# Strassen factors of a SwiGLU's w_down formed further ahead, and part of VectorE's work given to GpSimd

## The chip, the cores and the metric

The kernel runs on one core of a Trainium2 chip. The metric is the device time of one execution in microseconds: the median of three runs of the kernel before is 3245.2 us (3243.39 to 3246.24). TensorE (PE), VectorE (DVE), ScalarE (ACT) and GpSimd (POOL) each run their own list of instructions in a fixed order; SyncE (SP) and POOL issue the DMAs. An instruction that waits holds back everything behind it on its own engine.

## The reference

One layer of a decoder trunk on x of 2048 rows and 1024 columns, in float32, and a final norm:

```
h   = RMSNorm(x);  P = h @ W_in
A   = short gated convolution branch
B   = sparse attention: indexer scores I[t,s]; each query keeps the 256 best causal keys,
      softmax over them with a relative-position bias
m   = sigmoid(g_a) * y_a + sigmoid(g_b) * y_b
x   = x + m @ W_out
x   = x + (silu(h2 @ W_gate) * (h2 @ W_up)) @ W_down,   h2 = RMSNorm(x),  D_FF = 2816
out = RMSNorm_final(x)
```

The change concerns the last product, `@ W_down`, and the accumulation into x.

## The kernel before

The sequence is cut in two halves of 1024 rows. In order of time the program makes the projections and the indexer's scores for all rows, then for half 0 and after it for half 1: the attention, the branches and W_out, and the SwiGLU (MLP). The MLP of half 0 lies at about 1308 to 2029 us of the profiled run, that of half 1 at about 2535 to 3229 us.

Every float32 product is made of three matmuls on a high and a low part of each factor (`mm3`, L154). `split_w` (L128) makes the parts: ACT copies the high part (L129), and DVE or POOL subtracts it from the raw tile for the low part (L130).

The MLP takes the 22 tiles of 128 columns of D_FF in 11 pairs. `gate_up` (L932) computes one tile: 96 matmuls into PSUM tiles `gu`, a tanh on ACT (L945) and two operations on DVE (L946, L947) that leave the hidden tile `th`. The w_down product of a pair is a 2 by 2 block product, and for the first ten pairs it is made with seven products in place of eight (`PRODUCTS`, L975). Three of them (m3, m6, m5) are issued among the matmuls of the same pair's second gate_up, four (m2, m7, m4, m1) among those of the next pair's first one; `between` spreads them. Each product needs two factors: `hid`, a sum of two hidden tiles made by POOL (L964), and `wd`, a sum of two blocks of w_down made by DVE (L964), each then split in high and low (L129 on ACT, L130 on POOL for hid, on DVE for wd). The factors of one product are summed and split in one go, one product ahead. Each product has four PSUM tiles `dn` (four buffers), and DVE adds each of them to one or two blocks of the accumulator x2 (L1008). Since the products are shared out so, one block of x2 carries a combination of the others: `corner` (L1033) sets it up before the first pair and resolves it ahead of the last, by 12 operations on DVE each time (L1037). The last pair is made the ordinary way (L1064).

Half 0's MLP has a second task. The keys of the 128-row blocks 15 to 10, which half 1's attention needs, are selected by bisection as background work (priority lowered by `LOW`). Per block DVE prepares 16-bit keys (`descend_act`, L381 to L384), ACT runs 17 steps, each a sign count over the whole row (L358), then its sign (L367) and the next threshold (L369); DVE prepares the lower 16 bits (from L393 to L401), ACT runs 16 more steps, and DVE makes the threshold (L410 to L415) and the mask (`topk`, L425 to L448). Then the keys of the next block can follow. The first operations of half 1's attention (matmul L638, DVE L641) stand behind this on DVE.

The order on each engine is made by a scheduler from the order of emission and the priorities, so moving an emission moves instructions on several engines.

Of the kernel before, what the change touches and what calls it, by code (L numbers as in the profile page):

```python
# [25 lines left out]
P = 128  # L26
# [16 lines left out]
FB = 3  # L43
RAWB = (4, 4)
# [30 lines left out]
def trunk_kernel(tc, x, g_mix, w_in, b_gate, conv_w, w_a, w_b, w_out, rel_bias,  # L75
# [677 lines left out]
    for half in (0, 1):  # L753
# [206 lines left out]
        def combine(tag, bufs, eng, op, a, b=None):  # L960

            if b is not None:
                ab = ci.tile([P, CH], F32, name=tag, tag=tag, bufs=bufs)
                eng.tensor_tensor(ab, a, b, op=op)  # L964
                a = ab
            hi = ci.tile([P, CH], F32R, name=tag, tag=tag, bufs=bufs)
            lo = ci.tile([P, CH], F32R, name=tag, tag=tag, bufs=bufs)
            split_w(hi, lo, a, eng)
            return hi, lo
# [15 lines left out]
        def operands(name, A, B):  # L985

            def term(get, tag, bufs, eng, spec):
                if len(spec) == 1:
                    return combine(tag, bufs, eng, None, get(*spec[0]))
                return combine(tag, bufs, eng, spec[1], get(*spec[0]), get(*spec[2]))  # L990
            left, right = PRODUCTS[name][:2]
            return (term(lambda i, e: A[i, e], "hid", 8, nc.gpsimd, left),
                    term(lambda e, n: B[2 * e + n], "wd", 7, nc.vector, right))
# [39 lines left out]
        def corner(plus, minus):  # L1033

            for x0, x1 in zip(x2[0:4], x2[4:8]):
                for part, op in ((x1[:, 0:CH], plus), (x0[:, 0:CH], minus), (x0[:, CH:D], minus)):
                    nc.vector.tensor_tensor(x1[:, CH:D], x1[:, CH:D], part, op=op)  # L1037

        corner(ADD, SUB)
        held = None  # L1040
        for fpair in range(NF // 2):
# [4 lines left out]
            last = fpair == NF // 2 - 1  # L1046
            A, hid = {}, {}
            if held:
                begin(strassen(("m2", "m7", "m4", "m1"), *held), 16)
            if last:  # L1050
                gate_up(fpair, 0, lambda i, th: hid.update({(i, 0): combine("hid", 8, nc.gpsimd, None, th)}))
                drain()
                corner(SUB, ADD)
                B = down_rows(fpair)
                gate_up(fpair, 1, lambda i, th: hid.update({(i, 1): combine("hid", 8, nc.gpsimd, None, th)}))
                for n in range(2):
                    ns = slice(n * CH, (n + 1) * CH)
                    wd = [combine("wd", 7, nc.vector, None, B[2 * e + n]) for e in range(2)]
                    for tt in range(8):
# [5 lines left out]
                        if half == 1 and n == 1:  # L1065
                            finish(tt, x2[tt])
                break
# [6 lines left out]
            begin(strassen(("m3", "m6", "m5"), A, B), 12)  # L1074
# [44 lines left out]
```

## Time and profile before

| | |
|---|---|
| median of three runs | 3245.2 us |
| the profiled execution | 3246.63 us, its span 3244.9 us |
| PE busy | 3137.3 us, 97% of the span |
| DVE, ACT, POOL busy | 2154.5, 1947.2, 1023.0 us |
| mean granted clock of PE | 0.987 |

Busy shares are means over stages with different limits. In what follows a stage is read by its windows, by the waits of PE, and by the chain of ACT and DVE that the background search forms. A row of a timeline ends, where its engine stood idle, with the idle time and what ended it.

### The profile page before, as it was taken

To read this page: it belongs to the slowest core of one execution; us is meant where nothing else is said; L and a number is where in the kernel's file an instruction comes from. 1 tells how busy PE (TensorE), PEld (TensorE's weight loads), DVE (VectorE), ACT (ScalarE), POOL (GpSimd) and SP (SyncE) were. 2 spreads that over 40 slices of the span, in tenths; PEclk is the share of its full clock that TensorE was granted. 3 is DMA by queue.
4 is the path that set the end of the run, shared out by engine and by line. 5 is a ranking of instruction groups with operands and counts; after the bars stand their busy time and mean duration, and the time that the engine had idled before them with its cause. 6 is when DMAs were issued, how large, how long until landed. Compare 5 with 4: busy or idle time off the path is not lost. (4 is left out here: it accounts for less than half of the span.)

```text
span 3244.9 us, 42086 instructions
## 1 busy us (share of the span) xinstructions
PE 3137.3 (97%) x14483; PEld 2582.6 (80%) x14483; DVE 2154.5 (66%) x3762; ACT 1947.2 (60%) x3794; POOL 1023.0 (32%) x844
## 2 busy tenths in 40 slices
PE   8999999999999899899999999799999999999998
PEld 6788888888887678787878788587788788888886
DVE  6344356663527764878697987899863676667666
ACT  6479888779757785584848568677732322222222
POOL 5411122221114421344344433122221344344342
PEclk9999999999999999999999999899999999999999
DMA  7644333332334871322122225213372411111111
GB/s 226 178 136 127 94 95 97 96 99 90 104 112 108 221 256 46 92 68 87 51 84 70 89 63 140 71 53 79 102 248 65 143 65 53 46 59 46 46 46 52
DMA packets 338639, 324.82 MB, mean 100 GB/s; under 512 B 20340, under 2 KB 268360, under 8 KB 338040
## 3 DMA queue, kind: packets, MB, share of 16 engines
q1 hardware_dynamic: 301800, 293.64, 29.4%
q0 software_dynamic: 36624, 28.48, 4.3%
q8 instruction: 114, 1.87, 0.3%
q14 instruction: 101, 0.83, 0.1%
HBM read 248.09 MB, written 75.54 MB: 100 GB/s over the span
## 5 line engine op out<-in xcount | busy, mean ns | idle before, releaser
L1008 DVE SCALAR_TENSOR_TENSOR x<-dn,x 128x512 f32<-128x512 f32 x800 | 511.5, 683 | 201.4 <-PE dn L157 201.3
L358 ACT ACTIVATE dump<-key,nt 128x384 uint8<-128x384 int16 (+27 forms) x420 | 548.8, 1307 | 10.3
L155 PE MATMUL gu<-h2hi,wgu 128*128 128x512 f32 x1408 | 549.9, 391 | 0.1
L156 PE MATMUL gu<-h2lo,wgu 128*128 128x512 f32 x1408 | 549.2, 390 | 0.0
L157 PE MATMUL gu<-h2hi,wgu 128*128 128x512 f32 x1408 | 548.8, 390 | 0.0
L155 PE MATMUL mm<-hThi,whi 128*128 128x512 f32 (+2 forms) x1216 | 472.2, 389 | 1.2 <-ACT hThi L149 1.2
L157 PE MATMUL mm<-hThi,wlo 128*128 128x512 f32 (+2 forms) x1216 | 470.5, 388 | 0.8 <-POOL wlo L130 0.8
L156 PE MATMUL mm<-hTlo,whi 128*128 128x512 f32 (+2 forms) x1216 | 470.4, 387 | 0.0
L130 POOL TENSOR_TENSOR wlo<-raw,whi 128x512 fp32r<-128x512 f32 (+1 forms) x132 | 179.4, 1360 | 671.1 <-ACT whi L129 574.3
L266 DVE SCALAR_TENSOR_TENSOR acc<-r,iwT,acc 128x512 f32<-128x512 f32 (+2 forms) x266 | 196.2, 738 | 277.0 <-ACT r L261 275.7
L130 POOL TENSOR_TENSOR wgu<-raw,wgu 128x1024 fp32r<-128x1024 f32 x88 | 224.1, 2549 | 289.6 <-ACT wgu L129 280.9
L155 PEld LDWEIGHTS gu<-h2hi,wgu 128*128 128x128 f32 x1408 | 265.4, 188 | 56.1 <-DVE h2lo L150 0.7
L156 PEld LDWEIGHTS gu<-h2lo,wgu 128*128 128x128 f32 x1408 | 265.4, 189 | 55.1
L157 PEld LDWEIGHTS gu<-h2hi,wgu 128*128 128x128 f32 x1408 | 265.1, 188 | 55.3
L157 PEld LDWEIGHTS mm<-hThi,wlo 128*128 128x128 f32 (+1 forms) x1216 | 226.7, 187 | 50.6 <-POOL wlo L130 1.2
L155 PE MATMUL dn<-wd,hid 128*128 128x512 f32 x624 | 245.2, 393 | 17.8 <-ACT hid L129 10.3
L155 PEld LDWEIGHTS mm<-hThi,whi 128*128 128x128 f32 (+1 forms) x1216 | 226.8, 187 | 43.3 <-ACT hThi L149 1.4
L156 PEld LDWEIGHTS mm<-hTlo,whi 128*128 128x128 f32 (+1 forms) x1216 | 226.9, 187 | 42.6
L156 PE MATMUL dn<-wd,hid 128*128 128x512 f32 x624 | 244.5, 392 | 0.0
L157 PE MATMUL dn<-wd,hid 128*128 128x512 f32 x624 | 235.3, 392 | 1.1 <-POOL hid L130 1.0
L964 POOL TENSOR_TENSOR hid<-th 128x512 f32<-128x512 f32 x100 | 144.0, 1440 | 289.6 <-DVE th L947 282.9
L129 ACT ACTIVATE hid<-hid 128x512 fp32r<-128x512 f32 x100 | 62.8, 628 | 240.4 <-POOL hid L964 240.3
(210 smaller groups left out, 6315.0 us busy)
## 6 DMA issues: line engine op xcount, KB each, us to landing
raw<-in_w_in_dram SPq DMA_DIRECT2D x124, 256.0 KB
raw<-in_w_ffn_gate_dram SPq DMA_DIRECT2D x44, 512.0 KB
raw<-in_w_ffn_up_dram SPq DMA_DIRECT2D x44, 512.0 KB
rawd<-in_w_ffn_down_dram SPq DMA_DIRECT2D x44, 512.0 KB
S<-SD SPq DMA_DIRECT2D x80, 256.0 KB
GT<-f SPq DMA_DIRECT2D x64, 256.0 KB
ta<-GT SPq DMA_DIRECT2D x64, 256.0 KB
S<-SD SPq DMA_DIRECT2D x68, 192.0 KB
```

What stands on the lines that cost most here:

```text
L129: nc.scalar.activation(hi, raw, AF.Copy)
L130: lo_eng.tensor_tensor(lo, raw, hi.bitcast(F32), op=ALU.subtract)
L155: nc.tensor.matmul(ps, whi, xhi, start=start, stop=False)
L156: nc.tensor.matmul(ps, whi, xlo, start=False, stop=False)
L157: nc.tensor.matmul(ps, wlo, xhi, start=False, stop=stop)
L266: nc.vector.scalar_tensor_tensor(acc[:, 0:w], r[:, 0:w], wv, acc[:, 0:w], op0=ALU.mult, op1=ALU.add)
L358: nc.scalar.activation(dump, keys, AF.Sign, bias=nt, accum_out=sm)
L964: eng.tensor_tensor(ab, a, b, op=op)
L1008: nc.vector.scalar_tensor_tensor(acc, ps, 0.5 if op is ADD else -0.5, acc, op0=ALU.mult, op1=ALU.add)
```

## The change

Factors are now made in two steps. `factors` makes the sums for the product two ahead, `halves_of` the splits for the product one ahead; `ahead` decides at each of the four steps of a product what is due. The first sums and splits of a group are emitted when the group begins (`next(gen)` in `begin`), and the group of four products leaves out the first 6 of the 32 places of a gate_up and takes the rest at a higher rate. In half 0 the sums of w_down go to POOL (`SUMS`). `corner` runs on POOL, and its first call is emitted after the first gate_up instead of ahead of it.

```diff
-        def combine(tag, bufs, eng, op, a, b=None):
-            if b is not None:
-                ab = ci.tile([P, CH], F32, name=tag, tag=tag, bufs=bufs)
-                eng.tensor_tensor(ab, a, b, op=op)
-                a = ab
+        def halves_of(tag, bufs, eng, a):
             hi = ci.tile([P, CH], F32R, name=tag, tag=tag, bufs=bufs)
             lo = ci.tile([P, CH], F32R, name=tag, tag=tag, bufs=bufs)
             split_w(hi, lo, a, eng)
...
+        def factors(name, A, B):
+            both = []
+            for get, tag, bufs, eng, spec in ((lambda i, e: A[i, e], "hid", 8, nc.gpsimd, PRODUCTS[name][0]),
+                                              (lambda e, n: B[2 * e + n], "wd", 7, SUMS[half], PRODUCTS[name][1])):
+                whole = get(*spec[0])
+                if len(spec) > 1:
+                    whole = ci.tile([P, CH], F32, name=tag, tag=tag, bufs=bufs)
+                    eng.tensor_tensor(whole, get(*spec[0]), get(*spec[2]), op=spec[1])
+                both.append(whole)
+            return both
+
+        SUMS = (nc.gpsimd, nc.vector)
...
-            ops = [operands(names[0], A, B)]
+            whole, ops = [], []
+            def ahead(j):
+                while len(whole) < min(j + 2, len(names)) and all(x in A for x in PRODUCTS[names[len(whole)]][0][::2]):
+                    whole.append(factors(names[len(whole)], A, B))
+                while len(ops) < min(j + 1, len(whole)):
+                    left, right = whole[len(ops)]
+                    ops.append((halves_of("hid", 8, nc.gpsimd, left), halves_of("wd", 7, nc.vector, right)))
+            ahead(0)
+            yield
             for j, name in enumerate(names):
-                (hhi, hlo), (whi, wlo) = ops[j]
                 for t in range(4):
                     o = t * P
-                    if len(ops) == j + 1 < len(names) and all(x in A for x in PRODUCTS[names[j + 1]][0][::2]):
-                        ops.append(operands(names[j + 1], A, B))
+                    ahead(j if t == 0 else j + 1)
+                    (hhi, hlo), (whi, wlo) = ops[j]
...
-        def begin(gen, n):
+        def begin(gen, n, first):
             nonlocal due, rate
+            next(gen)
             steps.append(gen)
-            due, rate = 0.0, n / 32
+            rate = n / (32 - first)
+            due = -rate * first
...
-                    nc.vector.tensor_tensor(x1[:, CH:D], x1[:, CH:D], part, op=op)
-        corner(ADD, SUB)
+                    nc.gpsimd.tensor_tensor(x1[:, CH:D], x1[:, CH:D], part, op=op)
...
-                begin(strassen(("m2", "m7", "m4", "m1"), *held), 16)
+                begin(strassen(("m2", "m7", "m4", "m1"), *held), 16, 6)
...
+            if not held:
+                corner(ADD, SUB)
-            begin(strassen(("m3", "m6", "m5"), A, B), 12)
+            begin(strassen(("m3", "m6", "m5"), A, B), 12, 0)
```

POOL's list at the start of half 0's MLP, in the program before: `ms` and `rs` are the scalars of the RMSNorm, `wgu` the low parts of gate and up weights. The new program numbers its lines higher: L137 and L139 become L139 and L141, L1037 becomes L1051.

```order
L137 TENSOR_SCALAR ms<-ss 128x1
L139 TENSOR_TENSOR rs<-ms,nhalf 128x1
L137 TENSOR_SCALAR ms<-ss 128x1
L139 TENSOR_TENSOR rs<-ms,nhalf 128x1
L130 TENSOR_TENSOR hid<-th,hid 128x512
L130 TENSOR_TENSOR wgu<-raw_15347,wgu 128x1024
L130 TENSOR_TENSOR wgu<-raw_15557,wgu 128x1024
```

The same list in the changed program, from a scalar `ms` of one of the last norms on:

```order
L139 TENSOR_SCALAR ms<-ss 128x1
L1051 TENSOR_TENSOR x_12608<-x_12608,x_12506 128x512
L141 TENSOR_TENSOR rs<-ms,nhalf 128x1
L1051 TENSOR_TENSOR x_12610<-x_12610 128x512
L1051 TENSOR_TENSOR x_12610<-x_12610,x_12508 128x512
L1051 TENSOR_TENSOR x_12612<-x_12612 128x512
L139 TENSOR_SCALAR ms<-ss 128x1
L1051 TENSOR_TENSOR x_12610<-x_12610,x_12508 128x512
L1051 TENSOR_TENSOR x_12612<-x_12612,x_12510 128x512
L141 TENSOR_TENSOR rs<-ms,nhalf 128x1
```

Eight of the corner's operations now stand ahead of the last norm's `rs` (two of them, and a norm, ahead of the rows shown).

DVE's list in half 0, from the first operation that needs block 12's upper threshold (L393) on, in the program before; `x<-dn,x` are the accumulations (L1008), and the keys are made by L400 and L401:

```order
L393 TENSOR_SCALAR top<-nt 128x1
L395 TENSOR_SCALAR side<-nt 128x1
L405 TENSOR_SCALAR neg<-nt 128x1
L1008 SCALAR_TENSOR_TENSOR x_12506<-dn,x_12506 128x512
L397 TENSOR_SCALAR base<-side 128x1
L412 TENSOR_SCALAR turn<-neg 128x1
L398 TENSOR_SCALAR side<-side 128x1
L400 TENSOR_SCALAR dump<-key,top,side 128x512
L1008 SCALAR_TENSOR_TENSOR x_12508<-dn,x_12508 128x512
L407 TENSOR_SCALAR top<-top,side 128x1
L401 SCALAR_TENSOR_TENSOR key<-S,base,dump 128x512
```

The same place in the changed program, where L393 is L395, L400 is L402 and L1008 is L1020:

```order
L395 TENSOR_SCALAR top<-nt 128x1
L397 TENSOR_SCALAR side<-nt 128x1
L407 TENSOR_SCALAR neg<-nt 128x1
L1020 SCALAR_TENSOR_TENSOR x_12508<-dn,x_12508 128x512
L1020 SCALAR_TENSOR_TENSOR x_12610<-dn,x_12610 128x512
L1020 SCALAR_TENSOR_TENSOR x_12510<-dn,x_12510 128x512
L1020 SCALAR_TENSOR_TENSOR x_12612<-dn,x_12612 128x512
L399 TENSOR_SCALAR base<-side 128x1
L414 TENSOR_SCALAR turn<-neg 128x1
L1020 SCALAR_TENSOR_TENSOR x_12512<-dn,x_12512 128x512
L1020 SCALAR_TENSOR_TENSOR x_12614<-dn,x_12614 128x512
L400 TENSOR_SCALAR side<-side 128x1
```

Down to the last key operation of this block there are 7 operations of the MLP before and 21 now.

DVE's list at the end of half 0, in the program before and then in the changed one (L641 is L643 there, L410, L413, L415 and L425 are L412, L415, L417 and L427):

```order
L410 TENSOR_SCALAR li<-nt 128x1
L413 TENSOR_TENSOR li<-li,turn 128x1
L415 TENSOR_TENSOR thr<-li,top 128x1
L425 SCALAR_TENSOR_TENSOR dump,cnt_15148<-S,thr,zerob 128x512
L441 TENSOR_SCALAR eq<-S,thr 128x512
L641 ISA pr,mx<-lg,Mt 128x512
```

```order
L412 TENSOR_SCALAR li<-nt 128x1
L415 TENSOR_TENSOR li<-li,turn 128x1
L417 TENSOR_TENSOR thr<-li,top 128x1
L643 ISA pr,mx<-lg,Mt 128x512
L643 ISA mx 128x1
L427 SCALAR_TENSOR_TENSOR dump,cnt_15148<-S,thr,zerob 128x512
```

The first attention operation stands two instructions nearer to the threshold.

## Rows read from the trace of the kernel before

**Rows 1.** Busy time of each engine in three stretches: busy us (instructions), clock, DMA.

```profile
core 0: us, PE busy (x) PEld busy (x) DVE busy (x) ACT busy (x) POOL busy (x), PEclk, DMA share, GB/s
2020.00:2040.00 20.00, 8.88 (x40) 7.02 (x38) 6.46 (x14) 17.53 (x34) 2.02 (x4) 0.82 0.95 309
2700.00:2720.00 20.00, 20.00 (x90) 16.57 (x89) 13.51 (x18) 5.03 (x7) 9.63 (x6) 1.00 0.09 26
1280.00:2040.00 760.00, 725.88 (x3174) 595.80 (x3172) 616.43 (x994) 525.66 (x920) 305.73 (x196) 0.98 0.29 86
```

**Rows 2.** PE's timeline at half 0's end: start, duration, operation, idle time before.

```profile
2040.77 0.79 PE L638 MATMUL lg<-KH,q 128*128 128x512 f32 x1 [11.89 <-DVE mx L641]
```

**Rows 3.** ACT's timeline at the same place.

```profile
2038.05 0.29 ACT L369 ACTIVATE nt<-way,nt 128x1 f32<-128x1 f32 x1
```

**Rows 4.** DVE's timeline at the same place.

```profile
2038.37 0.15 DVE L410 TENSOR_SCALAR li<-nt 128x1 int32<-128x1 f32 x1 [8.76 <-ACT nt L369]
...
2038.95 0.75 DVE L425 SCALAR_TENSOR_TENSOR dump<-S,thr,zerob 128x512 bf16<-128x512 f32 x1
...
2040.02 0.69 DVE L641 CUSTOM_DVE_ANT_0 pr<-lg,Mt 128x512 f32<-128x512 f32 x1
```

**Rows 5.** Groups by line, 1280 to 2040 us: busy, mean ns, idle before.

```profile
L1008 DVE SCALAR_TENSOR_TENSOR x<-dn,x 128x512 f32<-128x512 f32 x400 | 255.1, 681 | 50.1 <-PE dn L157 50.0
...
L155 PE MATMUL dn<-wd,hid 128*128 128x512 f32 x312 | 124.1, 398 | 17.8 <-ACT hid L129 10.3 <-DVE x L1008 7.4
...
L964 POOL TENSOR_TENSOR hid<-th 128x512 f32<-128x512 f32 x50 | 74.8, 1496 | 158.0 <-DVE th L947 151.3 <-PE dn L157 6.7
...
L964 DVE TENSOR_TENSOR wd<-rawd 128x512 f32<-128x512 f32 x50 | 46.2, 924 | 3.3 <-DMA rawd<-in_w_ffn_down_dram 2.4
...
L129 ACT ACTIVATE hid<-hid 128x512 fp32r<-128x512 f32 x50 | 31.2, 624 | 82.7 <-POOL hid L964 82.6
...
L358 ACT ACTIVATE dump<-key,start_hi 128x1920 uint8<-128x1920 int16 (+4 forms) x5 | 8.4, 1679 | 32.3 <-DVE key L384 32.3
```

**Rows 6.** DVE's timeline at the start of half 0's MLP.

```profile
1303.05 1.28 DVE L1037 TENSOR_TENSOR x<-x,x 128x512 f32<-128x512 f32 x2
1304.25 1.28 DVE L140 SCALAR_TENSOR_TENSOR o<-x,rs,gB 128x1024 f32<-128x1024 f32 x1
...
1317.83 1.22 DVE L442 TENSOR_TENSOR_SCAN cs<-eq 128x512 f16<-128x512 bf16 x1
...
1328.26 3.41 DVE L442 TENSOR_TENSOR_SCAN cs<-eq,last 128x512 f16<-128x512 bf16 x1
1331.59 2.86 DVE L384 SCALAR_TENSOR_TENSOR key<-dump,key 128x512 int16<-128x512 bf16 x1
...
1338.75 0.67 DVE L384 SCALAR_TENSOR_TENSOR key<-dump,key 128x512 int16<-128x512 bf16 x1
```

**Rows 7.** DVE's timeline around block 12's second key preparation.

```profile
1724.93 0.15 DVE L393 TENSOR_SCALAR top<-nt 128x1 f32<-128x1 f32 x1
...
1737.16 0.62 DVE L401 SCALAR_TENSOR_TENSOR key<-S,base,dump 128x384 uint16<-128x384 uint16 x1
```

**Rows 8.** POOL's timeline at the start of half 0's MLP.

```profile
1291.08 0.55 POOL L139 TENSOR_TENSOR rs<-ms,nhalf 128x1 f32<-128x1 f32 x1
...
1327.75 2.84 POOL L130 TENSOR_TENSOR wgu<-raw,wgu 128x1024 fp32r<-128x1024 f32 x1
1331.51 2.39 POOL L130 TENSOR_TENSOR wgu<-raw,wgu 128x1024 fp32r<-128x1024 f32 x1 [0.93 <-ACT wgu L129]
```

**Rows 9.** DVE's groups by line and shape, 1280 to 2040 us.

```profile
L442 DVE TENSOR_TENSOR_SCAN cs<-eq,last 128x512 f16<-128x512 bf16 x8 | 13.4, 1672 | 0.0
...
L384 DVE SCALAR_TENSOR_TENSOR key<-dump,key 128x512 int16<-128x512 bf16 x11 | 11.2, 1018 | 0.0
```

**Rows 10.** PE's timeline in half 1's MLP.

```profile
2599.33 0.96 PE L157 MATMUL dn<-wd,hid 128*128 128x512 f32 x3 [1.02 <-POOL hid L130]
```

**Rows 11.** POOL's timeline at the same place.

```profile
2592.95 1.30 POOL L964 TENSOR_TENSOR hid<-th 128x512 f32<-128x512 f32 x1 [0.91 <-DVE th L947]
```

More of the change, by code (lines that the diff above doesn't have):

```diff
@@ L43 @@
 FB = 3
+SEVEN = (range(10), range(10))
 RAWB = (4, 4)
@@ L983, in trunk_kernel @@
         }
[L985 to L993, printed above, removed]
-        def strassen(names, A, B):
-            ops = [operands(names[0], A, B)]
+        def factors(name, A, B):
[9 more added lines that the diff above has]
+        SUMS = (nc.gpsimd, nc.vector)
+        def strassen(names, A, B):
+            whole, ops = [], []
[7 more added lines that the diff above has]
+            yield
             for j, name in enumerate(names):
-                (hhi, hlo), (whi, wlo) = ops[j]
                 for t in range(4):
                     o = t * P
-                    if len(ops) == j + 1 < len(names) and all(x in A for x in PRODUCTS[names[j + 1]][0][::2]):
-                        ops.append(operands(names[j + 1], A, B))
+                    ahead(j if t == 0 else j + 1)
+                    (hhi, hlo), (whi, wlo) = ops[j]
                     ps = dnp.tile([P, CH], F32, name="dn", tag="dn")
@@ L1045, in trunk_kernel @@
                 finish(fpair - 1, xt, (1, 0))
-            last = fpair == NF // 2 - 1
             A, hid = {}, {}
             if held:
-                begin(strassen(("m2", "m7", "m4", "m1"), *held), 16)
-            if last:
-                gate_up(fpair, 0, lambda i, th: hid.update({(i, 0): combine("hid", 8, nc.gpsimd, None, th)}))
+                begin(strassen(("m2", "m7", "m4", "m1"), *held), 16, 6)
+            if fpair not in SEVEN[half]:
+                gate_up(fpair, 0, lambda i, th: hid.update({(i, 0): halves_of("hid", 8, nc.gpsimd, th)}))
                 drain()
-                corner(SUB, ADD)
+                if held:
+                    corner(SUB, ADD)
+                    held = None
                 B = down_rows(fpair)
-                gate_up(fpair, 1, lambda i, th: hid.update({(i, 1): combine("hid", 8, nc.gpsimd, None, th)}))
+                gate_up(fpair, 1, lambda i, th: hid.update({(i, 1): halves_of("hid", 8, nc.gpsimd, th)}))
                 for n in range(2):
                     ns = slice(n * CH, (n + 1) * CH)
-                    wd = [combine("wd", 7, nc.vector, None, B[2 * e + n]) for e in range(2)]
+                    wd = [halves_of("wd", 7, nc.vector, B[2 * e + n]) for e in range(2)]
                     for tt in range(8):
@@ L1064, in trunk_kernel @@
                         nc.vector.scalar_tensor_tensor(x2[tt][:, ns], ps, 0.5, x2[tt][:, ns], op0=ALU.mult, op1=ALU.add)
-                        if half == 1 and n == 1:
+                        if half == 1 and n == 1 and fpair == NF // 2 - 1:
                             finish(tt, x2[tt])
-                break
+                continue
             gate_up(fpair, 0, lambda i, th: A.update({(i, 0): th}))
```

## The prediction

> **What bounds the kernel now.** I read the windows first, then the waits of PE, then the chain that ends each wait. In half 1's MLP the windows show PE busy for all 20.00 of 20 us with 90 matmuls at full granted clock, 0.222 us for each [rows 1]. There is no search beside it, and the only wait of PE on a factor that I find there is 1.02 us [rows 10]. So in half 1 the change has about one microsecond to win.
>
> Half 0's MLP is another matter. PE's waits in front of the w_down products add up to 17.8 us, 10.3 of them ended by the split of a hidden sum on ACT and 7.4 by an accumulation on DVE [rows 5]. That looks like the prize. The end of the half says otherwise: PE has done its last product and stands idle for 11.89 us until DVE's first attention operation [rows 2], and in the window around it PE is busy for 8.88 of 20 us while ACT is busy for 17.53 [rows 1]. Going back from that operation, DVE's L410 had waited 8.76 us for ACT's last threshold [rows 4], which ended at 2038.05 + 0.29 = 2038.34 [rows 3]. So the chain that sets the end of half 0 is the background search: ACT's steps for blocks 14 to 10, and between two blocks, and between a block's two halves of bits, the key and mask work on DVE. PE arrives 11.89 us before it is needed. A wait of PE inside the half costs nothing at the end until that slack is gone; what counts is how many MLP operations of DVE stand in front of the keys for which ACT waits. ACT's waits for first keys alone are 32.3 us [rows 5].
>
> **The change, part by part.** The unit is one MLP operation on DVE: they start 0.60 us apart when nothing holds them (two in 1.20 us, then L140) [rows 6], with a duration of 0.68 us.
>
> *First keys (L410 of one block to the last L384 of the next).* I count the MLP operations that DVE's order puts there, before and after. Block 14: 12 and 7, counted from the mask's first L425 (two corner operations, two sums and one accumulation go), 5 x 0.60 = -3.0. Block 13: 29 and 25, -2.4. Block 12: 39 and 28, -6.6. Block 11: 22 and 28, +3.6. Block 10: 14 and 14. Sum -8.4 us.
>
> *Second keys (L393 to the last L401).* Block 14: 8 and 15, +4.2. Block 13: 8 and 8. Block 12: 7 and 21, +8.4, on a stretch that lasts from 1724.93 to 1737.16 + 0.62, 12.9 us, now [rows 7]. Blocks 11 and 10: one less each, -1.2. Sum +11.4 us. The accumulations that now stand behind L393 had stood before it, where DVE had time while ACT searched. They can't start before L393, which waits for ACT, so they lie in the chain. From below, if their `dn` tiles come late from PE anyway, the chain waits longer still; from above, nothing lets them pass L393. I take +11.4.
>
> *ACT inside the search steps.* Between a block's first sign count and its last threshold, ACT's order has about two splits less over the five blocks: 2 x 0.62 = -1.2 us [rows 5].
>
> *The hand-over.* DVE's first attention operation now stands right behind the threshold, where the first mask operation L425 stood, instead of two operations later: 2038.95 - 2040.02 = -1.1 us [rows 4].
>
> *What POOL's new work does to DVE.* 50 sums go to POOL. They last 0.92 us on DVE and 1.50 us on POOL on the mean of half 0 [rows 5], 1.30 us where POOL is undisturbed [rows 11]; POOL has room, 305.73 of 760 us busy [rows 1]. But the two engines stretch each other. While POOL makes two weight parts that take 2.84 and 2.39 us [rows 8], DVE's scan takes 3.41 us against 1.22 and its key operation 2.86 against 0.67 [rows 6]. On the mean of the half these two forms take 1672 and 1018 ns [rows 9], so 8 x 0.45 + 11 x 0.35 = 7.4 us are lost in 19 instructions, 0.39 us each. The search has some 13 narrower ones of the two forms (5 us) and some 57 of three other forms with two inputs, which I take at half (11 us): 24 us for 305.73 us of POOL. 50 x 1.30 = 65 us more of POOL, 21%, make 5.0 us more. About 13 of the removed DVE sums lay in the chain and were themselves 0.23 us above the 0.69 us of an undisturbed operation: -3.0. Net +2.0 us. From below it is -3.0 (the new sums meet no search operation). From above, one search operation is stretched by the excess of these two rows, 2.2 us, for each of the 13 sums that move within the chain: 29 - 3 = +26. I stay near the mean, since it rests on many rows.
>
> The Trainium skill, "SBUF — State Buffer", section "Who interferes with whom", says that a DVE instruction with two SBUF inputs and a GpSimd instruction that reads SBUF exclude each other for a whole instruction, and that one with a single SBUF input is left alone. The trace agrees in kind: L384 reads two SBUF tiles and is stretched from 0.67 to 2.86 us, while L1008, with one input in PSUM, keeps a mean of 681 ns [rows 5, 6]. By that rule every one of the 13 sums could hold a search operation for its own length, an estimate of 17 us in place of 5.
>
> *The corner on POOL.* At the MLP's start eight of its operations stand ahead of the last norm's scalar rs on POOL. From the end of the fourth-last rs, 1291.08 + 0.55 [rows 8], 8 x 1.30 us [rows 11] and some 2.4 us of scalars give 1304.4, against the 1304.25 at which DVE's last L140 starts now [rows 6]. At POOL's mean of 1.50 it is 1306.0. DVE in turn is rid of its corner operations there. I take +1.0 us for each half, from -0.5 to +3. In front of the last pair 12 operations on POOL take 16 to 18 us, hidden by the last gate_up's 96 matmuls (21 us at 0.222), since the last pair's accumulations need x2 only after it; POOL's DMA issues behind them (the next attention's keys and queries) wait as long, and the matmuls before the 11.89 us gap cover it. Without that cover the price would be what is over, some 3 us.
>
> *PE's own waits.* Factors made earlier should take most of the 10.3 us behind ACT away. In half 0 that is worth nothing while the chain ends last. In half 1 it is -1.0 us [rows 10].
>
> **The sum.** Half 0: -8.4 + 11.4 - 1.2 - 1.1 + 2.0 + 1.0 = +3.7 us. Half 1: -1.0 + 1.0 = 0. The profiled execution took 3246.63 us (span 3244.9 and 1.7 around it), 1.4 above the median of the runs shown, so its 3250.3 is 3248.9 against 3245.2.
>
> **The rivals.** *A, the search gets shorter.* The +11.4 does not come, because what stands behind L393 only fills time in which the next key operation waited for its own input or for POOL, or because L393 is reached late on DVE and ACT already waits. Then half 0 has -8.4 - 3.0 - 1.2 - 1.1 + 1.0 = -12.7, half 1 up to -1: 3245.2 - 13.7 = 3231.5, and half of it, 3238, if half of the +11.4 comes. For it: in the stretch of 12.9 us [rows 7] a good part is more than the key operations' own time. Against it: the rows there leave DVE hardly an idle gap.
>
> *B, POOL and DVE hold each other.* The slower side. Its place is the key and mask work between two blocks, its price what one moved sum costs a search operation. At 1.3 us, a sum's whole length, 13 sums cost 17 us: +3.7 - 5.0 + 17 = +15.7, or 3261. It decides from about 0.6 us for each of the 13 (8 us, +6.7). For it: 2.86 against 0.67 us. Against it: the mean of 0.39 us.
>
> *C, the change does not do what it says.* The order on PE still puts the four-product groups in bunches, so the waits of 17.8 us stay. Since the search ends the half, the time would be that of the forecast, within a microsecond or two: 3246 to 3250.
>
> *D, PE is the bound after all.* If the search gave way by over 11.89 us, PE's removed waits would count, up to 17.8 - 11.89 = 6 us beyond A: 3225.
>
> **How the numbers follow.** About 0.2%, 6.5 us, is what a measurement of this kernel can tell from no change: 3238.7 to 3251.7. The forecast with C has 0.42, with its own range from 3239 to 3257 (+3.7, and the bounds of the corner and of half of POOL's price); A 0.28, D 0.05, B 0.25. Of the forecast's 0.42 about 0.33 lie within 0.2%, 0.06 above and 0.03 below; of A's 0.28 about 0.03 lie within. That makes faster 0.03 + 0.25 + 0.05 = 0.33, no change 0.33 + 0.03 = 0.36, slower 0.06 + 0.25 = 0.31. The range from 3229 to 3262 leaves out D, the stronger end of A and what is above B.
>
> **What would show it.** Right: the gap before the first L638 of half 1 still ended by L641 behind the search, larger than or near 11.89 us although the waits ended by ACT's hid splits are mostly gone; block 12's second keys at some 20 us; first keys shorter at blocks 14 and 12. Wrong: that gap down to a few microseconds (A or D), L384 and L442 in the mean well above 1.0 and 1.7 us (B), the same 10 us of waits on the hid splits (C).

## The result: slower by about 16 us

The changed kernel takes 3260.82 us (3258.11 to 3263.32, four runs) against 3244.3 for the kernel before (3241.33 to 3246.24, four runs on the same chip). The ratio is 1.0056, with an interval of 1.0044 to 1.0068. The forecast was 3248.9, which counts as no change; the time lies in the stated range, but it is 12 us above the sum, and it came about by other ways than the sum's.

The profiled execution has a span of 3257.6 us, 12.7 more than the one before. First the end of half 0, PE, ACT and DVE in the changed kernel, with the columns of [rows 2 to 4]:

```profile
2040.58 0.39 PE L159 MATMUL dn<-wd,hid 128*128 128x512 f32 x1
2050.04 0.79 PE L640 MATMUL lg<-KH,q 128*128 128x512 f32 x1 [9.07 <-DVE mx L643]
```

```profile
2048.50 0.29 ACT L371 ACTIVATE nt<-way,nt 128x1 f32<-128x1 f32 x1
```

```profile
2048.83 0.15 DVE L412 TENSOR_SCALAR li<-nt 128x1 int32<-128x1 f32 x1 [7.13 <-ACT nt L371]
...
2049.29 0.68 DVE L643 CUSTOM_DVE_ANT_0 pr<-lg,Mt 128x512 f32<-128x512 f32 x1
```

The picture is that of [rows 2 to 4], 10 us later: the search still ends the half, at 2048.8 in place of 2038.3, and the hand-over is 1.2 us shorter as forecast (2050.04 - 2048.79 = 1.25, before 2040.77 - 2038.34 = 2.43). And PE's own path grew as well: its last w_down product starts at 2040.58, 12.1 us later than before (2028.49). So two things went wrong in half 0 at once, and the gap in front of the attention shows only the one that ends last. Both are larger than these times say. Half 0's W_out, which lies ahead of what the change touches, ends at 1291.30 in this execution and at 1296.17 in the one before. Counted from there, PE's last product comes 17.0 us later, the search's end 15.3, and the end of the program 17.6.

The search's own part, from the starts and ends of its stretches on ACT. Waits for second keys: 13.5, 15.5, 13.7, 8.4, 7.0 us before, 20.0, 14.3, 22.8, 8.0, 6.6 now, +13.6 where the sum had +11.4. Waits for first keys of blocks 13 to 10: 48.1, 54.4, 39.3, 27.3 before, 47.0, 52.1, 43.0, 28.4 now, +1.2, and block 14's start 2.4 us later, counted from W_out's end: +3.6 where the sum had -8.4. DVE is idle for less than 1 us in each of these stretches, before and now, so their length is what DVE does in them. In the first-key stretches of blocks 13 to 10 the operations of the MLP take 73.1 us in place of 82.0, about what the count had promised, but those of the search take 121.5 in place of 112.0. In the second-key stretches the MLP's take 42.5 in place of 32.3, the search's 38.5 in place of 35.9. Block 12's second keys on DVE, to be held against [rows 7]:

```profile
1721.50 0.15 DVE L395 TENSOR_SCALAR top<-nt 128x1 f32<-128x1 f32 x1 [0.62 <-ACT nt L371]
...
1732.35 2.74 DVE L403 SCALAR_TENSOR_TENSOR key<-S,base,dump 128x384 uint16<-128x384 uint16 x1
...
1743.59 0.62 DVE L403 SCALAR_TENSOR_TENSOR key<-S,base,dump 128x384 uint16<-128x384 uint16 x1
```

22.7 us from the first row to the end of the last, 12.9 before: the 14 operations more are there, and one key operation (the middle row) takes 2.74 us where the last row's, of the same shape, takes 0.62.

PE's own part. Groups of the changed kernel, 1280 to 2050 us (columns as in [rows 5]):

```profile
L157 PE MATMUL dn<-wd,hid 128*128 128x512 f32 x312 | 126.5, 406 | 21.4 <-DVE x L1020 11.6 <-ACT hid L131 7.6 <-ACT wd L131 1.5
...
L159 PE MATMUL dn<-wd,hid 128*128 128x512 f32 x312 | 115.8, 397 | 3.3 <-POOL hid L132 3.3
```

Against [rows 5] the waits on hid splits by ACT fell from 10.3 to 7.6 us, but those on DVE's accumulations rose from 7.4 to 11.6 and new ones of 4.8 us came (POOL's low parts, w_down splits). The same can be read from the starts of the 3048 matmuls of half 0's MLP. From the first to the last they span 720.5 us before (1307.99 to 2028.49) and 733.7 now (1306.90 to 2040.58). At 0.2266 us from one to the next, their pace when nothing holds them, it would be 690.4: so 30.1 us were lost before and 43.2 now. Distances of over 0.5 us, the waits, make 22.9 and 29.9 us of that, shorter ones the rest. PE's first matmul of this MLP in the kernel before:

```profile
1307.99 0.79 PE L155 MATMUL gu<-h2hi,wgu 128*128 128x512 f32 x1
```

Then the start of the MLP, PE and then POOL in the changed kernel:

```profile
1297.79 3.67 PE L149 MATMUL gu<-ident,o 128*128 128x128 f32 x16 [4.74 <-DVE h2lo L152]
1305.31 1.94 PE L149 MATMUL gu<-ident,o 128*128 128x128 f32 x8 [3.85 <-DVE o L142]
1306.90 0.78 PE L157 MATMUL gu<-h2hi,wgu 128*128 128x512 f32 x1
```

```profile
1299.58 0.19 POOL L139 TENSOR_SCALAR ms<-ss 128x1 f32<-128x1 f32 x1
1299.85 2.49 POOL L1051 TENSOR_TENSOR x<-x,x 128x512 f32<-128x512 f32 x2
1302.30 0.55 POOL L141 TENSOR_TENSOR rs<-ms,nhalf 128x1 f32<-128x1 f32 x1
```

Two corner operations stand between the last norm's ms and rs, and DVE's L142 and PE wait for it. From the end of W_out's last matmul to the first gate_up matmul it is 15.6 us, before 11.8; in half 1 it is 15.05, before 13.03.

Last the operations of the search on DVE, by shape as in [rows 9]. Of the two forms shown there the scan rose from 1672 to 1809 ns and the key operation fell from 1018 to 856:

```profile
L444 DVE TENSOR_TENSOR_SCAN cs<-eq,last 128x512 f16<-128x512 bf16 x8 | 14.5, 1809 | 0.0
...
L386 DVE SCALAR_TENSOR_TENSOR key<-dump,key 128x512 int16<-128x512 bf16 x11 | 9.4, 856 | 0.0
```

These two alone would say that nothing got worse. Two others, before and then now:

```profile
L446 DVE SCALAR_TENSOR_TENSOR eq<-S,thr,eq 128x512 bf16<-128x512 f32 x13 | 11.1, 857 | 0.1
...
L384 DVE SCALAR_TENSOR_TENSOR key<-dump,key 128x384 int16<-128x384 bf16 x7 | 4.8, 684 | 0.0
```

```profile
L448 DVE SCALAR_TENSOR_TENSOR eq<-S,thr,eq 128x512 bf16<-128x512 f32 x13 | 14.4, 1109 | 0.0
...
L386 DVE SCALAR_TENSOR_TENSOR key<-dump,key 128x384 int16<-128x384 bf16 x7 | 8.0, 1147 | 0.1
```

All 343 operations that this search has on DVE take 196.6 us in sum before and 211.4 now. What separates the long from the short ones is POOL. 245 of them before and 219 now have no POOL instruction beside them in time, and each of these is within 0.03 us of the median of its form (that of the operations that run alone, over all kernels here). The 98 and 124 that have one are longer than that median by 47.0 and 62.2 us in sum, half a microsecond each. One form in the kernel before, alone and then beside POOL:

```profile
1808.11 0.43 DVE L381 TENSOR_SCALAR key<-S 128x512 uint16<-128x512 uint16 x1
```

```profile
1816.21 2.50 POOL L130 TENSOR_TENSOR wgu<-raw,wgu 128x1024 fp32r<-128x1024 f32 x1 [0.17 <-PE gu L157]
```

```profile
1816.37 2.62 DVE L381 TENSOR_SCALAR key<-S 128x512 uint16<-128x512 uint16 x1
```

So rival B's mark is in the trace: 15 us more of DVE time, 12.5 of them between block 14's second keys and block 10's, where the search waits for it.

### The profile page after: what moved, and what is told of

Same layout as the page of the kernel before. It is cut to its first block, busy times and chain, and to the rows that moved or that the text cites. A ratio compares the mean times of both kernels' runs of the same rounds, so it can differ in the third digit from the quotient of the medians.

```text
span 3257.6 us, 42125 instructions
## 1 busy us (share of the span) xinstructions
PE 3144.6 (97%) x14483; PEld 2586.8 (79%) x14483; DVE 2071.8 (64%) x3664; ACT 1946.9 (60%) x3794; POOL 1148.7 (35%) x942
## 4 chain that ended last, share of the span: by engine, by line
PE 72%; ACT 10%; DVE 8%; issue 4%; DMA 4%; POOL 2%; SPq 0%; POOLq 0%; DVEq 0%; ACTq 0%
PE mm L159 8%; PE mm L157 8%; PE mm L158 8%; PE gu L157 7%; PE gu L158 7%; PE gu L159 7%; ACT dump L360 5%; PE dn L157 4%; PE dn L158 4%; PE dn L159 4%; PE tpb L687 3%; PE sc L261 2%; PE sc L260 2%; PE lg L640 2%; PE pv L674 2%
## 5 line engine op out<-in xcount | busy, mean ns | idle before, releaser
L1020 DVE SCALAR_TENSOR_TENSOR x<-dn,x 128x512 f32<-128x512 f32 x800 | 508.7, 681 | 117.9 <-PE dn L159 117.0
L360 ACT ACTIVATE dump<-key,nt 128x384 uint8<-128x384 int16 (+27 forms) x420 | 548.8, 1307 | 10.3
L132 POOL TENSOR_TENSOR wgu<-raw,wgu 128x1024 fp32r<-128x1024 f32 x88 | 216.4, 2461 | 288.9 <-ACT wgu L131 285.7
L157 PE MATMUL dn<-wd,hid 128*128 128x512 f32 x624 | 247.6, 397 | 21.4 <-DVE x L1020 11.6
L157 PEld LDWEIGHTS mm<-hThi,whi 128*128 128x128 f32 (+1 forms) x1216 | 227.0, 187 | 42.5 <-ACT hThi L151 0.5
L263 ACT ACTIVATE r<-sc 128x512 f32<-128x512 f32 (+2 forms) x304 | 161.5, 532 | 60.3 <-PE sc L261 58.2
```

The costliest lines, as they stand in the source:

```text
L132: lo_eng.tensor_tensor(lo, raw, hi.bitcast(F32), op=ALU.subtract)
L157: nc.tensor.matmul(ps, whi, xhi, start=start, stop=False)
L263: nc.scalar.activation(r[:, 0:w], sc[:, 0:w], AF.Relu)
L360: nc.scalar.activation(dump, keys, AF.Sign, bias=nt, accum_out=sm)
```

## The experiments

Times are medians; the kernel before had 3242.1, 3241.9, 3243.2, 3242.3 and 3242.4 us in the five sets. A profile is one execution, and a kernel's runs lie 2 to 12 us apart, so verdicts go by the medians and their intervals, and profiles say only where.

**The parts of the change, one by one.** Theory 1: the search's chain is the bound, and what stands in front of its keys is the loss. Theory 2: POOL holds DVE's search operations.

```diff
e1: -        SUMS = (nc.gpsimd, nc.vector)
    +        SUMS = (nc.vector, nc.vector)
e2: corner on nc.vector, corner(ADD, SUB) again ahead of the loop over pairs
e3: e1 and e2 together
e4 (in the kernel before, combine):
    +            sums = nc.gpsimd if half == 0 else eng
    -                eng.tensor_tensor(ab, a, b, op=op)
    +                sums.tensor_tensor(ab, a, b, op=op)
```

> The changed kernel with half 0's sums of w_down back on VectorE (one word of SUMS). Theory 1, the background search sets half 0's end and pays for what VectorE's order puts in front of its keys: in this order 33 MLP operations stand behind the second-key starts of the five blocks, as against 31 before and 50 in the changed kernel, so the second keys get back to within 2 us of before (63 to 60, from 72 us of waits), while the first keys carry 23 operations more than in the changed kernel; half 0 ends 4 to 8 us later than in the kernel before, the time is 3249 to 3254. Theory 2, what costs is POOL's sums holding VectorE's search operations: the time falls back to the kernel before's apart from the corner's 2 us, 3244 to 3248, and the search's key and mask operations have the durations of before.

> The changed kernel with the corner back on VectorE and in its old place ahead of the first pair. Theory 1: the second keys of blocks 14 and 12 keep their 15 and 21 operations, so half 0 still ends 9 to 12 us later than before; half 1's MLP starts 2 us earlier, since the norm's scalars no longer wait on POOL: 3256 to 3260. Theory 2 (POOL's additional work is the cost): a third of the 74 additional POOL operations of half 0 goes, so a third of the 16 us: 3253 to 3256. A rival on the corner alone, that the scalars of the norm held up by the corner set both half starts: 3248 to 3252.

> The changed kernel with the sums of w_down and the corner both back on VectorE: what is left is the order, sums two ahead and splits one ahead. Theory 1: like the kernel with only the sums back, less 2 us for the corner: 3247 to 3252. Theory 2: 3242 to 3246, since PE's waits on the splits are fewer and POOL does no more than before.

> The kernel before with one change: half 0's sums of w_down are made by POOL, one product ahead as before. Counted in VectorE's order the first keys lose 14 MLP operations (-8.4 us at 0.60) and the second keys get 13 (+7.8). Theory 1 by the count: within 3 us of the kernel before, 3243 to 3249. Theory 2 (what POOL's sums do to VectorE is the cost): 50 POOL operations more, 10 to 14 us slower, 3254 to 3259, with the search's key and mask operations longer.

Measured: e1 3260.26, ratio 1.0052 (1.0039 to 1.0066); e2 3257.92, 1.0043 (1.0031 to 1.0056); e3 3252.24, 1.003 (1.002 to 1.004); e4 3252.75, 1.0029 (1.0017 to 1.004). So each part loses by itself: the order alone 10 us (e3), POOL's sums alone 11 (e4), the corner on POOL 8 on top of the order (e1 against e3), and together 16.5, less than their sum. Theory 1's numbers failed for e1 and e4, were met for e2, and missed by 0.2 us for e3; theory 2's failed for e1, e2 and e3, and in e4 its difference (10 to 14 us) was met. e4's profile has second-key waits of 67.7 us in place of 58.1, near the +7.8 of the count, while its first keys win 0.8 us in place of 8.4. PE's waits on hid splits are 14.5 us in place of 10.3; POOL's sums of w_down now stand in its queue too.

**Is the search the bound?** First with half of its steps left out (the masks are then coarse), then with the mask of a block made after the next block's keys.

```diff
e5 (before), e6 (after), blocks 15 to 10 only:
-        for bit in range(15, -1, -1):
+        for bit in range(15, 7, -1):
e7, e9 (before), e8, e10 (after):
-                for b in C_ACT[1:]:
-                    select_block_act(b)
+                for b in C_ACT[1:]:
+                    nxt = descend_act(b)
+                    topk(b + 1, thr, ...)   # scratch: an eq tile; two thr tiles
+                    thr = nxt
+                topk(C_ACT[-1], thr, ...)   # the last block's mask, after the loop
e9, e10 in addition:
-            TK["p"].tile([P, 112], F32, name="pad")
+            TK["p"].tile([P, 104], F32, name="pad")
```

> The kernel before with half of the search's steps: in each block of half 0's background search the two bisections stop at bit 8, so ACT makes 17 of 33 sign counts, and half 1's masks are coarse. Theory 1 (the search ends half 0): without some 5 x 16 x 2.5 = 200 us of chain, PE ends half 0; the gap of 11.89 us before half 1's first attention matmul goes down to 2 us or less, and the time falls by 8 to 20 us, to 3225 to 3237. Rival (PE and its waits on the factors end half 0): the time stays within 3 us of 3245.

> The changed kernel with the same half of the search's steps. Theory 1: with the search out of the way the loss of 16 us goes; what is left against the kernel before with the short search is the corner's 2 us in half 1's start and what PE's waits on factors give back in half 0, so -6 to +4 us. Theory 2 (POOL and VectorE hold each other, or the new order holds PE): the loss against the short-search kernel before stays at 10 us or more.

> The kernel before, with each block's mask emitted after the next block's keys, so that VectorE makes it while ACT searches on. Nothing is left out. Theory 1: the waits of ACT for first keys (48, 54, 39 and 27 us between blocks) lose the mask's 17 to 20 us each, the search ends before PE, the gap of 11.89 us goes down to 2 us or less: 3228 to 3237. Rival (PE ends half 0): 3243 to 3248.

> The changed kernel with the mask emitted after the next block's keys. Theory 1: the loss disappears, since the search no longer ends the half; 3226 to 3240, within 6 us of the kernel before with the same edit. Theory 2: 10 us or more slower than the kernel before with the same edit.

> The kernel before with each mask emitted after the next block's keys, as in the run without the alignment, and the pad tile cut from 112 to 104 floats, so that half 0's gate and up weight tiles keep their addresses (without that they lay 32 bytes lower and the matmuls of half 0's MLP were 0.232 us apart in place of 0.227). If the address is the cause of the wider pitch: pitch 0.227 again, 3054 x 0.0055 = 17 us less than with the unaligned tiles, 3221 to 3228. If it is not (the mask's new place slows the matmuls): 3237 to 3243 as before.

> The changed kernel with the same edit and the same pad. The search then ends 50 to 60 us before PE, so what is left between the two kernels is PE's own: Theory 3 (the moved sums and splits come later for PE in half 0, and the corner holds up the start of both halves, 3.8 and 2.0 us): 15 to 22 us slower than the kernel before with the same edit, 3238 to 3249. Theory 1 (the loss is the search's): within 6 us of it.

Measured: e5 3245.32, ratio 1.0016 (1.0006 to 1.0025); e6 3258.03, 1.0051 (1.0036 to 1.0066). In e5 ACT's last threshold and PE's next stage are:

```profile
1828.45 0.30 ACT L369 ACTIVATE nt<-way,nt 128x1 f32<-128x1 f32 x1
```

```profile
2040.95 0.39 PE L157 MATMUL dn<-wd,hid 128*128 128x512 f32 x1
2042.73 0.50 PE L638 MATMUL lg<-KH,q 128*128 128x512 f32 x1 [1.39 <-DVE mx L641]
```

The search ends 210 us earlier and the gap of [rows 2] is gone, as theory 1 said, yet no time is won: PE's last product comes 12.5 us later, since its waits on accumulations are 17.1 us in place of 7.4. Halving the steps brings DVE's key and mask work closer together and changes the whole order (the search's operations on DVE take 205.2 us in place of 196.6), so this was no clean removal of the chain. Theory 1's times failed in both. The rivals' were met: e5 is within 3 us of 3245, and e6 is 12.7 us above e5, where theory 2 had 10 or more.

e7 came out at 3240.01 (0.9999, 0.9989 to 1.0008), e8 at 3262.24 (1.0067, 1.0052 to 1.0082), but in both the matmuls of half 0's MLP followed each other more slowly, so e7 met neither theory. 20 us of it (columns as in [rows 1]) in e7 and in e9, the same kernel with the pad cut by 32 bytes:

```profile
1600.00:1620.00 20.00, 20.00 (x88) 16.15 (x87) 14.41 (x25) 18.03 (x31) 5.72 (x4) 1.00 0.14 42
```

```profile
1600.00:1620.00 20.00, 20.00 (x90) 16.57 (x89) 13.64 (x23) 18.82 (x33) 6.64 (x5) 1.00 0.13 37
```

With the smaller pad e9 takes 3230.6, ratio 0.9963 (0.995 to 0.9975), 12.6 us faster than the kernel before, and it is the fastest version here that leaves nothing out. That is between the two times expected: 9.4 us of the 17 came back. PE's last product is where it was and the gap is 1.39 us:

```profile
2027.87 0.39 PE L157 MATMUL dn<-wd,hid 128*128 128x512 f32 x1
2029.65 0.50 PE L638 MATMUL lg<-KH,q 128*128 128x512 f32 x1 [1.39 <-DVE mx L641]
```

So for the kernel before the forecast's reading was right: the search ended half 0, and taking it out of the way won the gap. For the changed kernel it was not enough: e10 takes 3257.78 (1.0048, 1.0035 to 1.006), no better than without the edit, though its search ends at 1989. PE's waits in e9 and then in e10:

```profile
L155 PE MATMUL dn<-wd,hid 128*128 128x512 f32 x312 | 125.0, 401 | 16.7 <-DVE x L1013 8.3 <-ACT hid L129 8.2
```

```profile
L157 PE MATMUL dn<-wd,hid 128*128 128x512 f32 x312 | 127.7, 409 | 31.0 <-ACT hid L131 18.5 <-DVE x L1025 12.1
```

The loss is 27 us with the search out of the way of half 0's end: theory 1 falls as the whole explanation of the loss. Theory 3 took its place: the moved operations make PE itself wait in half 0, and the corner holds up both starts. Its size was short too, 15 to 22 us expected. The search is out of the way of the end only, not off DVE: its 343 operations there take 199.6 us in e9 and 228.8 in e10.

**Without the search.** e11 and e12 leave the search of blocks 15 to 10 out and set their masks to zero.

> The kernel before without half 0's background search: the masks of blocks 15 to 10 are set to zero, so half 1 attends to every key of these blocks and the attention's work stays as it is. Half 0's MLP should then run like half 1's, 692 to 697 us in place of 720, and the time fall to 3212 to 3222 under any theory in which the waits in half 0 come from the search's work on VectorE and ScalarE.

> The changed kernel without half 0's background search, in the same way. Theory 3: PE's waits in half 0 come only together with the search's bursts on VectorE, so the loss shrinks to the corner's start costs, 4 to 7 us above the kernel before without search. Rival (the change loses by itself, in POOL's and ScalarE's order, search or not): 12 us or more above it.

Measured: 3217.58 (0.9922, 0.9909 to 0.9936) and 3223.18 (0.9938, 0.9923 to 0.9953), 5.6 us apart. As expected for both. PE's waits on the products are gone in both; in e11 and then in e12:

```profile
L155 PE MATMUL dn<-wd,hid 128*128 128x512 f32 x312 | 122.1, 391 | 0.1
```

```profile
L157 PE MATMUL dn<-wd,hid 128*128 128x512 f32 x312 | 122.1, 391 | 0.1
```

What remains is the corner. W_out's last matmul to the first gate_up takes 3.84 us more in half 0 and 2.02 in half 1, together 5.9. The remaining 11 us of the loss need the search beside the moved work. Both run half 0's matmuls at e7's slower pace (0.233 us, MLP 711 us long where 692 to 697 were expected), so they are to be compared with each other alone.

**Which part of the order.** The order-only kernel (e3) with one edit each; e15 and e16 with the later mask.

```diff
e13: -  while len(whole) < min(j + 2, len(names)) and ...
     +  while len(whole) < min(j + 1, len(names)) and ...
e14: -  begin(strassen(("m2", "m7", "m4", "m1"), *held), 16, 6)
     +  begin(strassen(("m2", "m7", "m4", "m1"), *held), 16, 0)
e15: e13 and e9's edit;  e16: e3 and e9's edit
```

> The kernel in which only the order is left of the change (sums of w_down and corner on VectorE), with the sums no further ahead than the splits, one product, as before; the delayed start of the four-product group and the first factors at the group's begin stay. VectorE's and POOL's orders are then those of the kernel before but for a few rows, and PE's has the three-product group evenly spread again (3 w_down matmuls between 6 to 11 others), while in the order-only kernel it begins 20 matmuls later and in runs of 6, 4 and 9. Theory 3a, the second product of lead costs, because it makes VectorE and POOL do sums ahead of what PE waits for next and bunches the three-product group: the 10 us of the order-only kernel go, within 3 us of the kernel before. Theory 3b, the delayed four-product group costs: it stays 7 to 12 us slower.

> The order-only kernel with two products of lead, but the four-product group spread over all 32 places again. Theory 3a: the loss stays, 7 to 12 us above the kernel before. Theory 3b: it goes, within 3 us of the kernel before.

> The kernel of e13 with each mask emitted after the next block's keys and the pad that keeps the weight addresses. Theory 3a: no slower than the kernel before with the later mask (3230.6), and up to 5 us faster if the smoother four-product group saves some of PE's 9 us of waits on hid splits: 3225 to 3232. Theory 3b: 3237 to 3243.

> The order-only kernel with the later mask and the pad. Theory 3a: 8 to 14 us above the kernel before with the later mask, 3238 to 3245. Theory 3b: the same, so that only the pair e13 and e15 tells the two apart; if it is within 3 us of 3230.6 the order is harmless once the search is short and the loss of the changed kernel with the later mask (27 us) is all POOL's.

Measured: e13 3244.18, ratio 1.0005 (0.9996 to 1.0014); e14 3253.06, 1.0033 (1.0021 to 1.0046); e15 3234.65, 0.9977 (0.9968 to 0.9987); e16 3241.15, 0.9994 (0.9985 to 1.0003). The second product of lead is what costs in the order: without it the loss is gone (e13), and with it the 10 us stay, delay or no delay (e14). With the later mask e16 is 10.5 us above e9 as expected. e15 lies between theory 3a and 3b: without the second lead 6.5 of these 10.5 us go, and the 4 us that stay are not explained. PE after its last product in e3 and in e13:

```profile
2044.64 0.79 PE L640 MATMUL lg<-KH,q 128*128 128x512 f32 x1 [8.75 <-DVE mx L643]
```

```profile
2034.24 0.80 PE L640 MATMUL lg<-KH,q 128*128 128x512 f32 x1 [11.87 <-DVE mx L643]
```

In both the search still ends the half. From the MLP's first matmul to the search's last threshold it is 730.4 us in the kernel before, 727.9 in e13, 741.8 in e3 and 747.5 in e14; to the end of PE's last product 720.9, 718.5, 728.7 and 728.6. So the second lead makes both paths longer, and in these kernels it is the search's that sets the time. PE's waits in e3, e13 and e14:

```profile
L157 PE MATMUL dn<-wd,hid 128*128 128x512 f32 x312 | 126.1, 404 | 18.9 <-DVE x L1020 11.0 <-ACT hid L131 6.1 <-ACT dump L360 1.3
```

```profile
L157 PE MATMUL dn<-wd,hid 128*128 128x512 f32 x312 | 124.1, 398 | 15.6 <-ACT hid L131 9.0 <-DVE x L1020 6.5
```

```profile
L157 PE MATMUL dn<-wd,hid 128*128 128x512 f32 x312 | 125.5, 402 | 19.4 <-DVE x L1020 12.7 <-ACT hid L131 6.4
```

The second lead does what it should to the hid splits (10.3 to 6.1 us), and raises the waits on accumulations from 7.4 to 11 or 12.7. In PE's order of half 0 the w_down matmuls of the first ten pairs stand in runs of six or more, two `dn` tiles and up, 20 times in the kernel before, 16 in e13, 28 in e3, 30 in e14 and 30 in the changed kernel. The waits on accumulations are 7.4, 6.5, 11.0, 12.7 and 11.6 us, so in these five they grow with the runs. But e5 has 23 runs and 17.1 us, e15 20 and 11.2, e16 26 and 8.3: that the runs cause the waits is not shown.

What goes with the times better is how much of the search on DVE lies beside POOL. From the traces, over the same 343 operations, how many have a POOL instruction beside them and by how much these are longer than the median of their form, with the median time against the kernel before of the same set:

| kernel | beside POOL | longer by, us | time, us |
|---|---|---|---|
| before | 98 | 47.0 | |
| e13, order without the second lead | 99 | 44.5 | +1.8 |
| e18, control of e17 | 96 | 46.7 | +7.4 |
| e3, order alone | 126 | 60.6 | +10.2 |
| e14, e3 without the delay | 111 | 57.9 | +10.7 |
| e4, POOL's sums alone | 122 | 58.3 | +10.7 |
| e2, order and POOL's sums | 119 | 64.7 | +15.9 |
| changed kernel | 124 | 62.2 | +16.5 |
| e1, order and corner | 122 | 59.0 | +18.2 |
| e17, changed, other buffers | 142 | 62.5 | +26.3 |
| e5 and e6, half the steps, before and changed | 135, 139 | 55.5, 73.4 | +3.4, +16.1 |
| e7 and e8, later mask, before and changed | 111, 155 | 55.2, 72.3 | -1.9, +20.3 |
| e9 and e10, the same with the smaller pad | 110, 159 | 50.3, 79.4 | -12.6, +14.6 |
| e15 and e16, e13 and e3 with the later mask | 115, 117 | 55.9, 59.7 | -7.7, -1.2 |

The order alone and POOL's sums alone bring 28 and 24 more operations beside POOL, and both together no more than that, which fits that their losses do not add up. e3 has no more work on POOL than the kernel before (297 and 294 us busy from 1300 to 2050 us), so there it is the order that decides, not the amount. e17 and e18 lose more than this explains. No run takes POOL's work away and leaves all else, so the share of this in the loss is read from traces and not shown by an experiment.

**Is it the factor buffers?** In the changed kernel POOL, ACT and DVE wait 77 us for a buffer of the w_down or hid factors that PE's products release, before 18.

```diff
e17 (after), e18 (before), half 0: "wd" bufs 7 -> 8, "eq" bufs 4 -> 3
```

> The changed kernel with eight buffers in place of seven for the w_down factors in half 0, paid for with one of the mask's four eq buffers. Theory 3c, factors made further ahead lie in wait for a buffer that PE's products release, and hold the engine behind them (77 us of such waits on POOL, ScalarE and VectorE in the changed kernel, 18 before): those waits fall to 50 us or less and the time by 4 to 10 us, to 3250 to 3256. Rival: the second product of lead costs by its order alone (bunched products, sums in front of the next split), buffers or not: within 3 us of the changed kernel, 3257 to 3262.

> The control: the kernel before with the same eight and three buffers. Both theories: within 4 us of the kernel before, 3238 to 3247, since only 18 us of its waits are for such buffers.

Measured: e17 3268.75, 1.0078 (1.0065 to 1.009); e18 3249.84, 1.0023 (1.0014 to 1.0033). No expectation was met. Those waits fall from 77 to 29 us, and nothing is won: the two kernels are 19 us apart, 16.5 without the edit, and the control itself loses 7 us. So theory 3c is not borne out. It is not cleanly refuted, since one eq buffer less and another order came together in the edit. Why e18 lost is open; its search is stretched by 46.7 us, no more than in the kernel before.

## Why the forecast was wrong

The reading of the bound was right for the kernel before, and e9 shows it: with the search out of the way 12.6 us go, about the gap of 11.89. That the time lies in the stated range is owed to rival B's share in that range and not to the sum. The steps that failed:

*What POOL's new work does to DVE, +2.0.* This is the step that failed most. The sum took a loss of 24 us in the kernel before and let it grow with POOL's busy time, by 21% or 5.0 us, less 3.0 for the sums that leave DVE. In the chain, from block 14's second keys to block 10's, the operations beside POOL are 53.0 us longer than the median of their form in the changed kernel and 40.5 in the kernel before: +12.5 in place of +5.0. The price of one was near (0.39 us there, about 0.5 here). How many there are was wrong: it does not follow POOL's busy time, since e3 and e1 have as many without POOL's sums of w_down. It follows the order, and that was counted in DVE's own queue and not for what runs beside it on POOL. +12.5 lies inside the step's own bounds of -3.0 to +26.

*First keys, -8.4.* The counts were right, and in the stretches of blocks 13 to 10 the MLP's operations did give back 8.9 us. But these stretches grew by 1.2 us, because the search's own operations in them grew by 9.5, the loss of the step above; and block 14's start came 2.4 us later in place of 3.0 earlier.

*"In half 0 that is worth nothing while the chain ends last"*, said of PE's own waits, and before it that factors made earlier take most of them away. What PE loses in half 0's MLP went from 30.1 to 43.2 us, and with the corner PE's last product comes 17.0 us later, more than the slack of 11.89. Had the search come as forecast, PE would have ended the half; and e10, in which it does, loses 27 us to e9. I counted what the lead takes from the hid splits (2.7 us in the profile) and nothing for what it does to the rest. Rival C named the bunches and priced them at nothing, because the search was to hide them. Why PE waits longer is in part open: in the changed kernel, e3 and e14 it waits more for DVE's accumulations, in e10 and e16 for ACT's splits of hid.

*The corner, +1.0 for each half.* It was mis-sized: 3.8 us in half 0, above its bounds of -0.5 to +3, and 2.0 us in half 1. I held the last norm's rs against DVE's last L140 alone; the corner also delays the norms ahead of it, and PE's transposes for these stand in line.

*Second keys, +11.4* measured +13.6, 10.2 of it by the MLP's operations; *ACT inside the search steps, -1.2* measured -1.9, *the hand-over, -1.1* measured -1.2; half 1's MLP is 0.6 us shorter where *half 1's wait* had -1.0. These were right.

Rival B had 3261, and its mechanism, POOL and DVE in each other's way at the search's keys and masks, is in the trace with 12.5 us of its 17. What it had wrong is that the moved sums bring it: e1 and e3 have the same without them on POOL. Its sign, L384 and L442 well above 1.0 and 1.7 us in the mean, was too narrow, because other forms took the loss. The Trainium skill, "SBUF — State Buffer", section "Who interferes with whom", says of a DVE instruction with at most one SBUF input that it does not contend with GpSimd outside the two-port performance modes. The prediction left that condition out. Here L381, with one input, takes 0.43 us alone and 2.62 beside POOL; in which mode it ran, no run shows.

In the profile, counted from half 0's W_out, half 1's first attention matmul is 14.1 us later (15.3 by the search less 1.2 at the hand-over), the last matmul of its W_out 15.7, its first gate_up matmul 17.7 (2.0 by the corner), and the end 17.6. The medians lie 16.5 apart.

## What to carry to other kernels

A slack read from one gap belongs to one path. Before calling another engine's waits free, ask whether the change can lengthen that path by as much as the slack; here two paths that ended 10 us apart both grew. Making operands earlier in an order that a scheduler writes also changes which operations run at the same time on two engines. An operation that DVE runs beside POOL took half a microsecond more here, in all kernels, and one more product of lead put 28 more of them there without any more work for POOL. A busy share of an engine does not tell this; count the pairs that overlap, over all forms and not only the two largest. Work that nobody needs soon, such as the masks here, is better put behind the next link of the chain than in front of it: that alone was worth 12.6 us.

## What was not expected of the hardware

The same matmuls were 0.232 us apart in e7 and 0.227 in e9, at a granted clock of 1.00 in both: 88 against 90 in 20 us, through the whole of half 0's MLP, and equal again in half 1. Between the two kernels 32 bytes of a pad tile differ, by which half 0's gate and up weight tiles start 32 bytes above a multiple of 64 (e7) or at one (e9). It made 9.4 us in the median, and would have been read as a failure of the later mask. The multiple of 64 is not the condition: in e11 and e12, whose programs are laid out otherwise, half 0's weight tiles start at multiples of 64 too, at other addresses than in e9, and the matmuls are 0.233 us apart as in e7. What the condition is stays open.

Of the 343 operations of the search on DVE none was longer than the median of its form by more than 0.03 us while POOL was silent, in any kernel here that has them; all that they lost, 44.5 to 79.4 us, they lost beside POOL.
